# A two-layer hybrid decoder trunk on one core: input sums of the fast FFN tiles emitted earlier, and four low weight parts per layer by accumulating transfers

## The chip, the cores and the metric

The kernel runs on one core of one Trainium2 chip. The metric is the device time of one execution in microseconds (us), lower is better. The profile's span is the time from the first to the last instruction of one profiled execution.

## The reference, cut to what matters

A trunk of two layers over 528 positions (16 learned ones, then 512 of input) and 1024 channels. Each layer normalises, mixes with three recurrent head groups, projects and adds; then it normalises again and runs a gated MLP with a short convolution. The change touches the MLP alone:

```
def conv_glu_ffn(h, w_up, conv_w, conv_b, w_down):
    u = causal_dwconv(jnp.einsum('btd,df->btf', h, w_up), conv_w, conv_b)   # 3 taps
    gate, val = jnp.split(u, 2, axis=-1)                                    # 2816 each
    return jnp.einsum('btf,fd->btd', jax.nn.silu(gate) * val, w_down)

for l in range(DEPTH):                                                      # DEPTH = 2
    h = h + hybrid_mixer(rmsnorm(h, norm_mix_g[l]), ...)
    h = h + conv_glu_ffn(rmsnorm(h, norm_ffn_g[l]), ffn_w_up[l], ffn_conv_w[l],
                         ffn_conv_b[l], ffn_w_down[l])
return rmsnorm(h, final_norm_g)[:, N_META:]
```

All of it is float32.

## The kernel before, in words

**Products.** Every float32 operand is cut in two parts of a shorter type, high and low, and a product is three matmuls: high by high, low by high, high by low (names end in h and l: `wh`, `wl` for weights, `xh`, `xl` for the normalised input, `ah`, `al` for activations, `th`, `tl` for the sums below). Activations lie with channels on the 128 partitions and positions along the free dimension, in two halves of 264 (258 in the second layer). A weight tile is 128x1024 (512 KB): eight blocks of 128 input channels.

**Cutting (`split`, L420 to L427).** ACT casts the source to the high part (L421). Then DVE subtracts it from the source (L427). With `by_dma` ACT writes the negated source, rounded, into the low part (L424) and POOL issues an accumulating transfer that adds the source to it (L425); DVE has no part in that.

**Weights.** `raw_src` lists what SP fetches in order, `items` what is cut, in the order of use. An item of kind `p` is cut with DVE, `q` by transfer. A raw tile lies in one of three buffers `raw` until its cutting is done, a cut tile in one of four pairs `wh`, `wl` until PE is done with it. `take()` hands out the next item and first emits the cutting of those up to three ahead (`prep(i + 3)`), which emits the fetches of those after.

**The MLP.** 22 tiles of 128 gate channels with 128 value channels, j = 0 to 21. Tiles 0 to 3 and 21 are plain (`up_pair`): a gate unit and a value unit, each with two halves of eight blocks of three matmuls. Tiles 0 and 1 run as one block of four units, first half and then second half. A half's result is copied from PSUM by ACT (L1035) and its last tap taken (L1005) into two buffers u and c; then DVE adds the other two taps (`conv`, L1000), ACT applies silu (L1017), DVE multiplies (L1022), and the product is cut into `ah`, `al`.

Tiles 4 to 20 are fast (`up_fast`, `pair_products`): a two by two scheme with seven block products in place of eight. It wants four sums of the normalised input per pair of channel blocks, called T1 to T4, for four pairs a = 0 to 3. `sum_pair(a)` makes them once per layer: DVE puts high and low together for both blocks (L1049, two buffers), makes T1 and T2 (L1055, L1056) and then T3 and T4 (L1059, L1060), a buffer for each two, and each is cut into `th`, `tl` by transfer. All these buffers, u, c and those of the sums, are of one tag `t` with seven buffers (`TM = 7`); one that a transfer reads is free when the transfer has landed. The fast tile uses T1 in its third product, T2 in its fourth, which adds onto the PSUM of its first, once ACT has copied that out (L1077), and T3 and T4 later. Between its products lie the down projection's units of the group of tiles before it; their weights come by the ring `rd` (256 KB) and are cut by transfer already.

**Order.** PE and SP run in the order in which the program is written. For DVE, ACT and POOL a scheduler settles the order when the program is built: an instruction emitted earlier goes first among those that are ready, and a buffer goes to the one that gets there first. On the chip each engine then keeps that order. `sum_pair(0)` is emitted behind tile 1, pairs 1 and 2 behind tile 2, pair 3 behind tile 3.

Of the kernel before, what the change touches and what calls it, by code (L numbers as in the profile page):

```python
# [19 lines left out]
KD = D // P  # L20
# [10 lines left out]
NFF = 22  # L31

GROUPS = ((0, 4), (4, 8), (8, 12), (12, 16), (16, 22))
FAST = range(4, 21)
DOWNS = ((), (2, 2, 2, 2), (2, 2, 2, 2), (2, 2, 2, 2), (2, 2, 2, 1, 1, 0))
TM = 7
Q0 = 12
MAXH = 2
# [55 lines left out]
def hybrid_trunk_kernel(ctx, tc, x, w_in, w_out, w_up, w_down, par, pre_in, lru_w, kon, msk, rope, out):  # L94
# [105 lines left out]
    raw_src, items = [], []  # L200
# [4 lines left out]
        group[f"x{j}"], group[f"y{j}"], group[f"s{j}"] = [M_LX + j], [M_LY + j], [M_RG + j]  # L205
    orders = [[m for k in o.split() for m in group[k]] for o in (ORDER, ORDER1)]

    def plain(src, kn, ring="raw"):
        raw_src.append((src, kn, ring))
        items.append(("p" if ring == "raw" else "q", len(raw_src) - 1, kn))  # L210

    for l in range(DEPTH):
        for m in orders[l]:
            plain(w_in[l, m], KD)
        for m in range(KD):
            plain(w_out[l, m], KD)

        for g, (k0, k1) in enumerate(GROUPS):
            rows = iter(range(KD))
            for i, j in enumerate(range(k0, k1)):  # L220
                down = [next(rows) for _ in range(DOWNS[g][i] if g else 0)]
                if j in FAST:
                    raw_src.extend((w_up[l, r], KD, "raw") for r in (j, NFF + j))
                    ri = len(raw_src) - 2
                    items.extend((k, ri, KD) for k in "ab")
                    for q, m in enumerate(down):
                        plain(w_down[l, m, :, slice(*GROUPS[g - 1]), :], 4, "rd")
                        if q == 0:
                            items.append(("c", ri, KD))
                    if not down:  # L230
                        items.append(("c", ri, KD))
                    items.append(("d", ri, KD))
                else:
                    plain(w_up[l, j], KD)
                    plain(w_up[l, NFF + j], KD)
        for m in range(KD):
            plain(w_down[l, m, :, k0:k1, :], k1 - k0)
    raws, ready, sums = {}, {}, {}
# [256 lines left out]
    def whole(hi, lo):  # L495
        return lambda t0, n: (hi[:, t0:t0 + n], lo[:, t0:t0 + n])
# [406 lines left out]
    def layer(l):  # L903
# [86 lines left out]
        phase[0].release()  # L990
        phase[0], n_t[0] = tc.alloc_tile_pool(name=f"mlp{l}", bufs=1), TM
        c0 = META if lastl else 0
# [33 lines left out]
        def up_pair(j):  # L1026
            us = {}

            def ev(key, m):

                def f(i, t0, n, ps):
                    if key not in us:
                        us[key] = new_u()
                    u, c = us[key]
                    S.copy(u[:, 2 + t0:2 + t0 + n], ps[:, 0:n])  # L1035
                    o = max(t0, c0)
                    tap(u, c, m, o, t0 + n, ps[:, o - t0:n])
                return f
            return [(None, ev("g", j), lambda: gate(j, us)), (None, ev("v", NFF + j), lambda: value(j, us))]
# [4 lines left out]
        def sum_pair(a):  # L1044

            y = []
            for k in (2 * a, 2 * a + 1):
                y.append(big())
                V.tensor_tensor(y[-1][:, 0:2 * hn], xh[:, k, h0:T].bitcast(F32), xl[:, k, h0:T].bitcast(F32), op=ALU.add)  # L1049
            (b11, b12), (b21, b22) = ((t[:, 0:hn], t[:, hn:2 * hn]) for t in y)  # L1050
            for i in (0, 2):
                t = big()
                p0, p1 = t[:, 0:hn], t[:, hn:2 * hn]
                if i == 0:
                    V.tensor_tensor(p0, b11, b12, op=ALU.subtract)  # L1055
                    V.scalar_tensor_tensor(p1, p0, -1.0, b22, op0=ALU.mult, op1=ALU.subtract)  # L1056
                    t2 = p1
                else:
                    V.tensor_tensor(p0, b22, b12, op=ALU.subtract)  # L1059
                    V.scalar_tensor_tensor(p1, t2, -1.0, b21, op0=ALU.mult, op1=ALU.subtract)  # L1060
                split(t[:, 0:2 * hn].rearrange("p (h t) -> p h t", t=hn), *(x[:, a, i:i + 2, 0:hn] for x in tsum),
                      by_dma=True)
# [7 lines left out]
        def up_fast(j, halves):  # L1070
            us = {k: new_u() for k in "gv"}
            ug, uv = (us[k][0][:, 2 + h0:2 + T] for k in "gv")

            def evac(what, ps):
                p = ps[:, 0:hn]
                if what == "c11":
                    S.copy(ug[:, 0:hn], p)  # L1077
                elif what == "u":
                    S.copy(ug[:, hn:2 * hn], p)
                elif what == "q5":  # L1080
                    S.activation(uv[:, hn:2 * hn], p, AF.Copy, scale=-1.0)
                elif what == "c11b":
                    V.tensor_tensor(ug[:, 0:hn], ug[:, 0:hn], p, op=ALU.add)
                elif what == "c12":
                    V.tensor_tensor(ug[:, hn:2 * hn], ug[:, hn:2 * hn], p, op=ALU.add)  # L1085
                    u, c = us["g"]
                    tap(u, c, j, c0, T, u[:, 2 + c0:2 + T])
                    gate(j, us)
                elif what == "v":
                    V.tensor_tensor(uv[:, hn:2 * hn], uv[:, hn:2 * hn], p, op=ALU.subtract)  # L1090
                else:
                    S.activation(uv[:, 0:hn], p, AF.Copy, scale=-1.0)
                    u, c = us["v"]
                    tap(u, c, NFF + j, c0, T, u[:, 2 + c0:2 + T])
                    value(j, us)
            cut_at = (len(halves) + 1) // 2

            def between(i):
                for f in (halves[:cut_at], halves[cut_at:])[i]:
                    f()  # L1100
            pair_products(xs_fast, KD // 2, hn, evac, between)

        def down_halves(m, xs):

            w = []

            def f(t0, n):
                if not w:
                    w.append(take())
                ps = ps_mm.tile([P, 512], F32, tag="mm", name=nm("mm"))  # L1110
                product(w[0], xs, t0, n, range(len(xs)), ps, True, True)
                resid(m)(0, t0, n, ps)
            return [lambda t0=t0, n=n: f(t0, n) for t0, n in hd]

        for g, (k0, k1) in enumerate(GROUPS):
            rows = iter(range(KD))
            prev = [whole(*act[k]) for k in range(*GROUPS[g - 1])] if g else []
            for i, j in enumerate(range(k0, k1)):
                halves = [f for _ in range(DOWNS[g][i] if g else 0) for f in down_halves(next(rows), prev)]
                if j in FAST:  # L1120
                    up_fast(j, halves)
                else:
                    if j == 0:
                        run_units([u for i_ in range(2) for u in up_pair(i_)], xs_norm, hv, first=4)
                    elif j > 1:
                        run_units(up_pair(j), xs_norm, hv)
                    if j in (1, 2, 3):
                        for a in {1: (0,), 2: (1, 2), 3: (3,)}[j]:
                            sum_pair(a)

        def final(t0, n):
# [27 lines left out]
    with tc.manual_schedule(engines={mybir.EngineType.PE, mybir.EngineType.SP}):  # L1159
# [132 lines left out]
        for l in range(DEPTH):  # L1292
            layer(l)
# [106 lines left out]
```

## Time and profile before

| | us |
|---|---|
| median of 3 runs (1286.71 to 1287.97) | 1287.32 |
| the profiled execution | 1288.41 |
| its span | 1286.5 |
| PE busy | 1258.5 (98%) |
| DVE busy | 988.6 (77%) |
| ACT busy | 752.0 (58%) |
| POOL busy | 79.5 (6%) |
| mean granted clock of TensorE | 0.987 |

Busy times are sums over the span. The first layer's MLP runs from about 276 us, its first fast tile from about 324; in the second layer these are about 910 and 958. The granted clock is a share of full speed: 1.00 is 2.4 GHz and 0.50 is 1.2 GHz.

### The profile page before, as it was taken

Reading aid. Unit: us, or ns where it says so; the run is one execution under the profiler, and the core shown is the slowest. Engines: PE = TensorE matmul, PEld = TensorE weight load, DVE = VectorE, ACT = ScalarE, POOL = GpSimd, SP = SyncE. Lnnn points to the kernel's source line nnn. Section 1 sums busy time; section 2 is a strip of 40 time slices with the busy share of each in tenths; the row PEclk is TensorE's granted clock in tenths of the full one; section 3 lists DMA queues with packets and bytes.
Section 4 is the critical chain, followed back from the end, with each engine's and each line's share of the span. In section 5 each row is a group of like instructions: output and inputs, shape, how many; then the busy total and the mean of one; then the engine's idle time right before and its main releaser. Section 6 shows DMA issues by size and latency. Waiting matters only on the chain.

```text
span 1286.5 us, 25758 instructions
## 1 busy us (share of the span) xinstructions
PE 1258.5 (98%) x10244; PEld 1245.9 (97%) x10244; DVE 988.6 (77%) x1946; ACT 752.0 (58%) x1442; POOL 79.5 (6%) x179
## 2 busy tenths in 40 slices
PE   9999999999899999999999999999999999999997
PEld 8999999999899999999999999999989999999996
DVE  7987676468788888887588767764896888888865
ACT  6665555347666666666456645553684666666652
POOL 0000000001211111100000000000021111111000
PEclk8999999999899999999999999999998999999998
DMA  5322312324555445544232223122265555555422
GB/s 197 98 78 67 100 50 66 99 67 122 126 132 132 131 128 136 132 124 115 75 99 67 66 66 100 50 83 66 87 136 139 132 132 131 132 137 135 111 88 74
DMA packets 53240, 135.32 MB, mean 105 GB/s; under 512 B 5632, under 2 KB 12288, under 8 KB 53120
## 3 DMA queue, kind: packets, MB, share of 16 engines
q1 hardware_dynamic: 39424, 110.46, 27.5%
q0 software_dynamic: 12544, 21.06, 9.7%
q10 hardware_dynamic: 1152, 2.16, 0.5%
q8 instruction: 80, 1.31, 0.4%
q14 instruction: 40, 0.33, 0.1%
HBM read 110.51 MB, written 2.10 MB: 88 GB/s over the span
## 4 chain that ended last, share of the span: by engine, by line
PE 86%; DVE 6%; ACT 3%; DMA 3%; issue 1%; SPq 0%; POOL 0%; DVEq 0%; ACTq 0%; POOLq 0%
PE mm L130 63%; PE mx L130 23%; DMA tl<-t 2%; DVE t L1000 1%; PE mx L137 1%; DVE wl L427 1%; DVE t L567 1%; DVE t L1138 0%; DMA raw<-in_w_in_dram 0%; DVE sc L591 0%; ACT wh L421 0%; ACT th L421 0%; DMA mk<-in_msk_dram 0%; DVE t L870 0%; ACT sc L674 0%
## 5 line engine op out<-in xcount | busy, mean ns | idle before, releaser
L130 PE MATMUL mm<-xh,wh 128*128 128x264 f32 (+1 forms) x1424 | 417.9, 293 | 0.8 <-ACT xh L421 0.8
L130 PE MATMUL mm<-xl,wh 128*128 128x264 f32 (+1 forms) x1424 | 404.3, 284 | 0.7 <-DVE xl L427 0.3
L130 PE MATMUL mm<-xh,wl 128*128 128x264 f32 (+1 forms) x1424 | 403.4, 283 | 0.0
L130 PE MATMUL mm<-ah,wh 128*128 128x264 f32 (+2 forms) x960 | 273.2, 285 | 0.0
L130 PEld LDWEIGHTS mm<-xl,wh 128*128 128x128 f32 x1424 | 268.8, 189 | 3.7 <-issue 1.9
L130 PE MATMUL mm<-al,wh 128*128 128x264 f32 (+2 forms) x960 | 272.4, 284 | 0.0
L130 PE MATMUL mm<-ah,wl 128*128 128x264 f32 (+2 forms) x960 | 272.1, 283 | 0.0
L130 PEld LDWEIGHTS mm<-xh,wh 128*128 128x128 f32 x1424 | 268.5, 189 | 3.6 <-issue 2.0
L130 PEld LDWEIGHTS mm<-xh,wl 128*128 128x128 f32 x1424 | 268.6, 189 | 0.2 <-DVE wl L1195 0.2
L427 DVE TENSOR_TENSOR wl<-raw,wh 128x1024 fp32r<-128x1024 f32 (+2 forms) x168 | 182.5, 1088 | 82.2 <-ACT wh L421 81.7
L421 ACT CAST wh<-raw 128x1024 fp32r<-128x1024 f32 (+2 forms) x168 | 158.3, 942 | 149.2 <-PE mm L130 143.6
L130 PEld LDWEIGHTS mm<-ah,wh 128*128 128x128 f32 x960 | 182.0, 190 | 0.1
L130 PEld LDWEIGHTS mm<-al,wh 128*128 128x128 f32 x960 | 181.9, 189 | 0.1
L130 PEld LDWEIGHTS mm<-ah,wl 128*128 128x128 f32 x960 | 181.9, 189 | 0.0
L1000 DVE SCALAR_TENSOR_TENSOR t<-t,pr,t 128x528 f32<-128x528 f32 (+1 forms) x176 | 132.7, 757 | 11.1 <-ACT t L1005 5.1
L130 PE MATMUL mx<-th,wh 128*128 128x264 f32 (+1 forms) x408 | 117.2, 287 | 0.0
L130 PE MATMUL mx<-th,wl 128*128 128x264 f32 (+1 forms) x408 | 116.6, 286 | 0.0
L130 PE MATMUL mx<-tl,wh 128*128 128x264 f32 (+1 forms) x408 | 116.3, 285 | 0.0
L1005 ACT ACTIVATE t<-t,pr 128x528 f32<-128x528 f32 (+1 forms) x68 | 56.0, 823 | 58.5 <-DVE t L1085 56.5
L427 DVE TENSOR_TENSOR wl<-ss,wh 128x1024 fp32r<-128x1024 f32 x68 | 83.0, 1221 | 4.6 <-ACT wh L421 1.8
L425 POOL DMA_DIRECT2D wl<-rd x64 | 56.6, 884 | 448.6 <-ACT wl L424 384.4
L130 PEld LDWEIGHTS mx<-tl,wh 128*128 128x128 f32 x408 | 78.3, 192 | 0.0
(231 smaller groups left out, 2170.9 us busy)
## 6 DMA issues: line engine op xcount, KB each, us to landing
raw<-in_w_up_dram SPq DMA_DIRECT2D x88, 512.0 KB, 3.6
raw<-in_w_in_dram SPq DMA_DIRECT2D x52, 512.0 KB, 3.6
rd<-in_w_down_dram SPq DMA_DIRECT2D x64, 256.0 KB, 2.7
wl<-rd POOLq DMA_DIRECT2D x64, 256.0 KB, 3.6
raw<-in_w_out_dram SPq DMA_DIRECT2D x16, 512.0 KB, 3.5
raw<-in_w_down_dram SPq DMA_DIRECT2D x16, 384.0 KB, 3.1
hT<-in_x_dram SPq DMA_DIRECT2D x4, 528.0 KB, 5.4
t<-in_rope_dram ACTq DMA_DIRECT2D x8, 264.0 KB, 3.3
```

Of the source, the lines that this page charges most:

```text
L130: PE.matmul(o, a, b, start=start, stop=stop, **kw)
L137: PE.transpose(o, a, ident[0:n, 0:n])
L421: S.copy(hi, src)
L425: G.dma_start(lo, src, accum_op=ALU.add)
L427: V.tensor_tensor(lo, src, hi.bitcast(F32), op=ALU.subtract)
L567: V.tensor_tensor(o, a, b, op=ALU.mult)
L1000: V.scalar_tensor_tensor(c[:, 0:cn], u[:, i + c0:i + c0 + cn], pr[l][:, w + i:w + i + 1], c[:, 0:cn], op0=ALU.mult, op1=ALU.add)
L1005: S.activation(c[:, a - c0:b - c0], src, AF.Identity, bias=pr[l][:, C_FB + m:C_FB + m + 1], scale=pr[l][:, C_FW + 3 * m + 2:C_FW + 3 * m + 3])
```

## The change

`sum_pair` of pairs 0 and 1 is emitted behind tile 1, of pairs 2 and 3 behind tile 2, and none behind tile 3. The gate and value weights of tiles 2 and 3 (four tiles of 128x1024 per layer) become items of kind `q`: their low part is made by ACT's negated copy and an accumulating transfer of 512 KB. They stay on the ring `raw`.

```
+SENT = (2, 3)
...
-    def plain(src, kn, ring="raw"):
+    def plain(src, kn, ring="raw", by_dma=False):
         raw_src.append((src, kn, ring))
-        items.append(("p" if ring == "raw" else "q", len(raw_src) - 1, kn))
+        items.append(("q" if by_dma else "p", len(raw_src) - 1, kn))
...
-                        plain(w_down[l, m, :, slice(*GROUPS[g - 1]), :], 4, "rd")
+                        plain(w_down[l, m, :, slice(*GROUPS[g - 1]), :], 4, "rd", True)
...
-                    plain(w_up[l, j], KD)
-                    plain(w_up[l, NFF + j], KD)
+                    plain(w_up[l, j], KD, by_dma=j in SENT)
+                    plain(w_up[l, NFF + j], KD, by_dma=j in SENT)
...
-                    if j in (1, 2, 3):
-                        for a in {1: (0,), 2: (1, 2), 3: (3,)}[j]:
+                    if j in (1, 2):
+                        for a in {1: (0, 1), 2: (2, 3)}[j]:
                             sum_pair(a)
```

## Rows read from the trace of the kernel before

**Rows 1.** The page's first part: busy time of each engine, its share of the span and the count of instructions.

```profile
PE 1258.5 (98%) x10244; PEld 1245.9 (97%) x10244; DVE 988.6 (77%) x1946; ACT 752.0 (58%) x1442; POOL 79.5 (6%) x179
```

**Rows 2.** PE's waits over the whole span, longest first: who waited for what, us in total, how often, the longest.

```profile
PE mm L130 <- DMA tl<-t: 9.0, 2, 4.8
PE mm L130 <- ACT th L421: 2.5, 2, 1.5
PE mx L130 <- DVE acc L442: 2.0, 2, 1.2
```

**Rows 3.** The timeline of PE at the first fast tile, two rows of each layer: start, duration, the instruction, and in brackets the idle time before it and what ended it.

```profile
329.41 0.39 PE L130 MATMUL mm<-th,wh 128*128 128x264 f32 x1 [1.04 <-ACT th L421]
334.03 0.59 PE L130 MATMUL mm<-tl,wh 128*128 128x264 f32 x1 [4.23 <-DMA tl<-t]
...
962.82 0.39 PE L130 MATMUL mm<-th,wh 128*128 128x258 f32 x1 [1.46 <-ACT th L421]
967.98 0.58 PE L130 MATMUL mm<-tl,wh 128*128 128x258 f32 x1 [4.78 <-DMA tl<-t]
```

**Rows 4.** Windows around the first fast tile in both layers: the stretch and its length, busy time and instructions of PE, weight loads, DVE, ACT and POOL, granted clock, DMA share, GB/s.

```profile
292.00:328.00 36.00, 36.00 (x299) 36.00 (x298) 34.22 (x54) 29.07 (x54) 6.58 (x11) 1.00 0.55 133
...
334.00:339.05 5.05, 5.02 (x23) 5.02 (x24) 0.69 (x1) 1.29 (x3) 0.05 (x1) 0.50 0.59 101
339.05:345.00 5.95, 5.95 (x50) 5.95 (x50) 3.10 (x6) 2.23 (x3) 0.00 (x0) 0.99 0.51 147
...
968.00:974.00 6.00, 6.00 (x28) 6.00 (x29) 0.74 (x2) 1.28 (x3) 0.00 (x0) 0.50 0.71 134
974.00:980.00 6.00, 6.00 (x52) 6.00 (x52) 3.83 (x7) 2.81 (x3) 0.00 (x0) 0.99 0.41 117
```

**Rows 5.** The chain of work that ended last, two pieces of 300 to 340 us and one of 935 to 975: start, length, what.

```profile
309.81 5.58 DMA tl<-t
...
330.23 3.75 DMA tl<-t
...
963.59 4.35 DMA tl<-t
```

**Rows 6.** Windows of 6 us ahead of the first fast tile of the first layer; the columns are those of rows 4.

```profile
300.00:306.00 6.00, 6.00 (x52) 6.00 (x51) 5.96 (x10) 3.97 (x8) 0.10 (x1) 1.00 0.51 164
306.00:312.00 6.00, 6.00 (x52) 6.00 (x51) 6.00 (x12) 5.28 (x11) 1.96 (x3) 1.00 0.43 106
312.00:318.00 6.00, 6.00 (x51) 6.00 (x51) 6.00 (x10) 3.28 (x7) 0.00 (x0) 1.00 0.81 204
318.00:324.00 6.00, 6.00 (x52) 6.00 (x51) 6.00 (x13) 5.93 (x13) 2.38 (x5) 1.00 0.53 90
324.00:330.00 6.00, 4.76 (x37) 4.34 (x36) 6.00 (x11) 6.00 (x13) 2.33 (x5) 1.00 0.77 134
```

**Rows 7.** The timeline of DVE: the first and the last of the four subtractions for the weights of tiles 2 and 3 in the first layer, the first of what stands ahead of pair 3's L1056 there, and that L1056 in both layers.

```profile
293.33 1.22 DVE L427 TENSOR_TENSOR wl<-raw,wh 128x1024 fp32r<-128x1024 f32 x1 [2.38 <-ACT wh L421]
...
308.26 1.21 DVE L427 TENSOR_TENSOR wl<-raw,wh 128x1024 fp32r<-128x1024 f32 x1
...
323.26 0.67 DVE L292 TENSOR_TENSOR ss<-raw 128x512 f32<-128x512 f32 x1
323.86 0.75 DVE L1000 SCALAR_TENSOR_TENSOR t<-t,pr,t 128x528 f32<-128x528 f32 x1
...
328.14 0.43 DVE L1056 SCALAR_TENSOR_TENSOR t<-t,t 128x264 f32<-128x264 f32 x1
...
961.68 0.42 DVE L1056 SCALAR_TENSOR_TENSOR t<-t,t 128x258 f32<-128x258 f32 x1
```

**Rows 8.** Groups of ACT's instructions from 292 to 329 us, shapes kept apart: busy us, mean ns of one, idle time before them.

```profile
L421 ACT CAST wh<-raw 128x1024 fp32r<-128x1024 f32 x5 | 5.2, 1050 | 2.9 <-PE mm L130 2.9
L421 ACT CAST th<-t 128x528 fp32r<-128x528 f32 x7 | 4.4, 629 | 2.7 <-DVE t L1056 2.7
...
L424 ACT ACTIVATE tl<-t 128x528 fp32r<-128x528 f32 x6 | 3.9, 643 | 0.0
```

**Rows 9.** Accumulating transfers into tl: the issues on POOL and the time from issue to landing over the whole span (16 transfers), then landing times of those issued from 308 to 310, from 942 to 945 and from 323 to 327 us (two each).

```profile
L425 POOL DMA_DIRECT2D tl<-t x16: 856/1090/1632, 308.7 to 965.8; - x16
DMA to landing us min/median/max: 3.3/3.8/6.6
...
DMA to landing us min/median/max: 5.2/5.4/5.6
...
DMA to landing us min/median/max: 6.0/6.3/6.6
...
DMA to landing us min/median/max: 3.3/3.3/3.4
```

**Rows 10.** The timeline of ACT in the first layer: the casts of tile 2's weights, which wait for a buffer that PE gives up, and a cast of a sum.

```profile
292.25 1.05 ACT L421 CAST wh<-raw 128x1024 fp32r<-128x1024 f32 x1 [1.79 <-PE mm L130]
...
295.17 1.05 ACT L421 CAST wh<-raw 128x1024 fp32r<-128x1024 f32 x1 [1.12 <-PE mm L130]
...
317.69 0.63 ACT L421 CAST th<-t 128x528 fp32r<-128x528 f32 x1 [2.72 <-DVE t L1056]
```

**Rows 11.** SP's issues of weight fetches in the first layer, the first and the last of four: start, duration, what.

```profile
294.58 0.33 SPq L249 DMA_DIRECT2D raw<-in_w_up_dram  x1
...
309.53 0.33 SPq L249 DMA_DIRECT2D raw<-in_w_up_dram  x1
```

## The prediction

> **What bounds the kernel now.** I read the page's busy shares first: PE is busy for 98% of the span [rows 1]. So the only time to be had, short of fewer matmuls, is the little that PE waits and the time in which it runs at its lower clock. The list of PE's waits comes next [rows 2]. Of its entries two belong to the place that the change touches: 9.0 us for a transfer into tl and 2.5 us for the cast into th, two waits each, which is one per layer. They are 11.5 us of PE's idle time, and every other entry is 2.0 us or less.
>
> The timeline of PE shows where they lie [rows 3]. In layer 0 the first fast tile (tile 4) starts its T1 product; its first three row pairs run, then PE waits 1.04 us for th of the last pair, does one matmul, and waits 4.23 us for tl of the same pair. In layer 1 the same two waits take 1.46 and 4.78 us. In stretches around them the granted clock falls [rows 4]: from 334.00 to 339.05 it is 0.50, the lower of the two levels (1.2 of 2.4 GHz), and 23 matmuls take 5.05 us, where 50 take 5.95 us right behind it. 23 × 0.119 = 2.74 us, so 2.31 us are lost. In layer 1 it is 0.50 from 968 to 974, 28 matmuls in 6.00 us against 52 in 6.00: 28 × 0.115 = 3.23, so 2.77 us are lost. Waits and clock together are 11.5 + 5.1 = **16.6 us**: the most that this change can return, unless it touches something else.
>
> Why the last tl is late I read from the chain of waits in that stretch [rows 5] and the windows of 6 us [rows 6]: DVE is busy 6.00 of 6.00 us in each one from 306 to 330, while ACT has 2.72 us to spare in 312 to 318. The chain goes through DVE's convolutions (L1000) and the sums (L1055, L1056) and ends in a 3.75 us transfer issued at 330.23. It holds a second transfer, 5.58 us from 309.81: a "t" buffer (there are seven) that pair 1 needed was held until pair 0's tl had landed. So the wait has three parts in series: DVE's backlog, buffers held by transfers, the last transfer itself.
>
> **The change part by part.**
>
> *Low parts off DVE.* The weights of tiles 2 and 3 are four per layer. Each loses one DVE subtraction, 1.22 us, at 293.33, 296.25, 301.17 and 308.26 in layer 0 [rows 7]: 4 × 1.22 = 4.9 us off an engine that is the bottleneck from about 299 on. The first two lie partly beside idle DVE time (2.38 us idle before the first), but the later two don't, and the convolutions behind the first two start earlier as far as ACT lets them.
>
> *Sums ahead of tiles.* Pair 1's sums now precede tile 2, pair 3's precede tile 3, in priority on DVE, ACT and POOL. Ahead of pair 3's L1056 (328.14) DVE now does three convolution steps of tile 3 (323.86, 325.14, 327.46, spaced 0.68) and two weight sums of tile 5 (0.60 each) [rows 7]: 2.0 + 1.2 = 3.2 us that can go behind it. By DVE alone, then, this sum ends at 328.57 − 4.9 − 3.2 = 320.5.
>
> *ACT.* Each of the four gets a negated copy of 128x1024. The trace has none of that size; the casts of that size take 1050 ns, and at 128x528 the negated copy (643 ns) is as long as the cast (629 ns) [rows 8]. So 4 × about 1.0 = 4.1 us more work. ACT is busy 29.07 of the 36 us from 292 to 328 [rows 4]; it would be 33.1. The cover is thin, so I take nothing for it on PE, but part of it as a delay of the sums (below). Bounds: nothing lost, if the copies fall into the 6.9 idle us, to all 4.1 us late.
>
> *Four transfers of 512 KB.* None of this kind and size is in the trace. From both sides: a single one of 264 KB lands 3.3 us after its issue at best, 6.6 at worst; two of them issued together (528 KB, 308.75) land after 5.2 and 5.6 us, in layer 1 after 6.0 and 6.6 [rows 9]. The pair is nearest, so 6.0 us, with 3.3 to 13.2 (twice the worst) as ends. First use: the cast of tile 2's first weight runs at 292.25, its copy would end at 294.3, its transfer land at 300.4. PE frees a buffer every 2.92 us (292.25, 295.17) [rows 10], so eight half units of 2.92 us end at 292.2 + 3 × 2.92 = 301.0 and tile 2 begins there, wanting this low part with its third matmul at 301.3. The margin is 0.9 us. The next three land near 304, 308 and 312 and are wanted at 307, 313 and 319; their margins grow. Cost on PE: nothing; price if it is late: the lateness, plus about 2.5 us if the clock falls.
>
> *SP's queue.* A raw buffer (there are three) is now freed when its transfer lands and no longer when DVE's subtraction ends. The fetches at 294.58, 297.50, 302.41 and 309.53 [rows 11] move to about 300, 304, 308 and 312, and the two fetches of tile 4's partner rows behind the third move with it. The last weight of tile 3 is then cast near 305 and wanted at 319, tile 4's weights at 324.5 and 327: hidden. POOL issues four more transfers; behind one that still waits for ACT stand the tl transfers of pairs 0 and 1, which are not ready before 306.
>
> *The last transfer.* From L1056's end to the issue of its tl transfer are 330.23 − 328.57 = 1.7 us. I add 3 us to 320.5 for "t" buffers and ACT together: each pair holds two for a transfer's length, pairs 0 and 1 want eight in a row and there are seven, and the one such hold that the chain shows is 5.6 us against a DVE that had other work. So issue at 325.2; a landing of 5.0 us (the middle of 3.3 and 6.6) gives 330.2. PE wants th at 329.41 − 1.04 = 328.4 [rows 3] and tl right after. **A wait of 1.8 us is left** where 5.27 were, and in layer 1, worked in the same way (L1056 ends at 962.1, the issue is 1.5 us later at 963.59 [rows 5, 7]; 962.1 − 4.9 − 3.2 + 3 + 1.5 + 5.0 = 963.5, against 962.82 − 1.46 = 961.4 with 0.1 for the matmul between), 2.0 us where 6.24 were. Whether a wait of 2 us lowers the clock no row here shows; a wait of 1.04 us stands alone for only one matmul. I take that it does not.
>
> The Trainium skill ("DMA: Bandwidth & Descriptors", section on the anatomy of a SWDGE DMA) has a fit of 2.0 us plus the bytes over 436 GB/s; as an estimate from it 264 KB land after 2.6 us, and then no wait would be left and the sum would be the full 16.6 us. The trace disagrees: its fastest such transfer takes 3.3 us.
>
> What is late next, if this wait is gone, is T2, which needs the copy out of the first product (L1077), done at 329.80 on an ACT that was full; with 328.7 as its new due time this is within a microsecond and part of the same 1.8.
>
> **Sum.** 16.6 − 1.8 − 2.0 = 12.8 us. The profiled execution took 1288.41 us, of which 1286.5 are the span; 1288.41 − 12.8 = 1275.6. It lies 1.09 above the median of the runs, so against 1287.32 the forecast is **1274.5 us**.
>
> **The rivals.**
>
> *ACT takes DVE's place.* For it: 33.1 of 36 us busy, and ACT's order is fixed, so an idle stretch that waits for DVE (2.72 us at 317.69 [rows 10]) is not simply filled. Against: the four copies are early, at 293 to 306, and the window from 300 to 306 has 2.0 us free [rows 6]. If the whole 4.1 us come back as delay, layer 0's last tl lands at about 331 to 332 rather than 330.2, the wait is some 3 us, and the clock falls as it does now: each layer returns 2 to 3.5 us. 1287.3 − 6 = 1281.
>
> *Nothing comes of it: the buffers.* Seven "t" buffers for two pairs in a row (eight) and tile 2's four: tile 2's results must leave PSUM by 312.8, when the fifth half unit from there wants one of four PSUM buffers. If pairs 0 and 1 hold all seven past that, PE waits there instead, and a wait of about 4 us with its clock only moves. 1287. For it: the hold in the chain [rows 5]. Against: tile 0's and tile 1's buffers come free from 296 to 307, and only four can hang on a transfer at a time.
>
> *Slower: the transfers follow one another too slowly.* PE uses one of the four weights per 5.85 us. If a 512 KB transfer takes 8.5 us and they go one behind the other, the first is 1.5 us late and each of the next three 2.65 more: 9.5 us, with a fall of the clock 12 per layer. The sums get that time too, so the 8.3 us of now are gone: +3.7 per layer, 1295. It decides from 5.85 us per transfer on. For it: two of 264 KB took 6.6 us in layer 1. Against: that includes the fixed part, and in 318 to 327 single ones landed after 3.3 us [rows 9].
>
> The Trainium skill ("SBUF — State Buffer", "SBUF: two separate sides") says that DVE in a two-port mode locks GpSimd out and starves such transfers of descriptors. By that rule the transfers would be slowest just where DVE is full, and the slower case would be the likeliest. The trace speaks against it: with DVE busy 6.00 of 6.00 us from 318 to 330, POOL's issues took 0.86 to 1.2 us and landings 3.3 us.
>
> **How the numbers follow.** Forecast 0.62 (own range 1270 to 1279), ACT 0.16, the buffers 0.10, slower 0.12. Less than all of 16.6 us can hardly be beaten: 1287.3 − 16.6 = 1270.7, so the low end is 1270. The high end takes in the ACT case with its spread, 1285; the rest, 0.2, lies above. What this kernel's runs can tell from no change is 0.2%, 2.6 us: faster 0.78, within 0.09 (most of the buffers case), slower 0.13.
>
> **What would show it.** Right: PE's waits on tl and th fall from 11.5 us to under 5, the granted clock stays at 1.00 behind the start of tile 4, DVE has no subtraction into wl from raw between 293 and 309, and pair 3's L1056 ends by 324. Wrong: a PE wait on a transfer wl<-raw at tile 2's start (first step of the 512 KB part); a PE wait on t or a PSUM evacuation by ACT near 313 (buffers); pair 3's th waiting on ACT work with DVE idle (ACT); or a wait of the old length with the sums ahead of it done early, which would mean that the transfer alone, and not DVE's backlog, set it.

## The result, and the profile after

The changed kernel takes 1302.91 us (median of 3 runs, 1302.85 to 1303.00) against 1287.32: a ratio of 1.0121, 95% interval 1.0098 to 1.0144. It is slower by 15.6 us; the forecast was 1274.5. Its profiled execution has a span of 1301.1 us, 14.6 more than before. Where these lie is in the first part of the page (busy time, share of the span and instructions of each engine), which answers to [rows 1]:

```profile
PE 1264.0 (97%) x10244; PEld 1250.3 (96%) x10244; DVE 981.1 (75%) x1938; ACT 758.9 (58%) x1450; POOL 86.3 (7%) x187
```

PE has the same 10244 instructions, is busy 1264.0 − 1258.5 = 5.5 us longer, and is idle 37.1 us (1301.1 − 1264.0) where it was 28.0: 9.1 + 5.5 = 14.6. The longer busy time goes with the clock: it is 0.66 to 0.90 in the last four windows below, where [rows 6] have 1.00 in each. DVE lost its eight subtractions and ACT gained eight copies, as said, so the load did move. PE's waits over the span (who waited for what, us in total, times, longest), against [rows 2]:

```profile
PE mm L131 <- DMA wl<-raw: 9.6, 2, 5.2
PE mm L131 <- ACT t L1006: 6.3, 3, 2.7
PE mx L131 <- DVE dg L466: 2.4, 2, 1.2
...
PE mm L131 <- DMA tl<-t: 1.9, 1, 1.9
...
PE mm L131 <- ACT ah L422: 1.5, 1, 1.5
```

(Most line numbers are one higher than before: L131 was L130, L422 was L421, L1006 was L1005.) The 11.5 us of waits for th and tl have come down to 1.9. In their place stand two waits that the kernel before did not have: a low part made by transfer, once per layer, and results leaving PSUM (L1006), those of tile 2 in the first layer. The timeline of PE shows them in the first layer and the first of them in the second; they lie a tile and more ahead of the place of [rows 3]:

```profile
311.42 0.59 PE L131 MATMUL mm<-xh,wl 128*128 128x264 f32 x1 [4.37 <-DMA wl<-raw]
322.01 0.39 PE L131 MATMUL mm<-xh,wh 128*128 128x264 f32 x1 [2.67 <-ACT t L1006]
...
953.52 0.58 PE L131 MATMUL mm<-xh,wl 128*128 128x258 f32 x1 [5.24 <-DMA wl<-raw]
```

The windows of 6 us over the stretch that [rows 6] show before (columns as there: PE, weight loads, DVE, ACT, POOL, granted clock, DMA share, GB/s):

```profile
300.00:306.00 6.00, 6.00 (x52) 6.00 (x51) 5.64 (x10) 4.36 (x9) 0.00 (x0) 1.00 0.32 87
306.00:312.00 6.00, 1.63 (x11) 1.42 (x10) 4.31 (x10) 6.00 (x11) 4.15 (x5) 0.77 0.71 131
312.00:318.00 6.00, 6.00 (x37) 6.00 (x36) 0.00 (x0) 1.65 (x4) 1.99 (x5) 0.66 1.03 184
318.00:324.00 6.00, 3.33 (x24) 3.11 (x23) 2.48 (x4) 3.46 (x7) 0.00 (x0) 0.90 1.07 276
324.00:330.00 6.00, 6.00 (x43) 6.00 (x43) 5.60 (x12) 2.47 (x5) 0.00 (x0) 0.81 0.69 205
```

PE does 11, 37 and 24 matmuls in three windows where it did 52, 51 and 52. DVE, 6.00 us busy in each of them before, does nothing at all from 312 to 318. And the DMA engines, 0.32 busy from 300 to 306, are full from 312 on. An idle DVE beside full transfers is the opposite of the shortage that the change set out to mend: the work waits for data, and the data waits for something that came late.

What came late stands in the timeline of ACT:

```profile
293.83 1.05 ACT L425 ACTIVATE wl<-raw 128x1024 fp32r<-128x1024 f32 x1
295.06 1.05 ACT L422 CAST wh<-raw 128x1024 fp32r<-128x1024 f32 x1 [0.17 <-PE mm L131]
...
299.19 1.04 ACT L422 CAST wh<-raw 128x1024 fp32r<-128x1024 f32 x1
...
303.88 1.05 ACT L422 CAST wh<-raw 128x1024 fp32r<-128x1024 f32 x1 [1.64 <-DMA raw<-in_w_up_dram]
304.85 0.63 ACT L1018 ACTIVATE t<-t 128x528 f32<-128x528 f32 x1
305.38 1.99 ACT L425 ACTIVATE wl<-raw 128x1024 fp32r<-128x1024 f32 x2
...
309.94 1.04 ACT L425 ACTIVATE wl<-raw 128x1024 fp32r<-128x1024 f32 x1
...
320.44 1.04 ACT L422 CAST wh<-raw 128x1024 fp32r<-128x1024 f32 x1 [6.79 <-DMA raw<-in_w_up_dram]
321.39 1.03 ACT L1006 ACTIVATE t<-mm,pr 128x264 f32<-128x264 f32 x2
```

L422 is a weight's cast, L425 its negated copy. The first copy stands close behind its cast. The second and third do not: the casts of their weights end at 296.1 and 300.2, the copies run at 305.38, behind the fourth cast and a silu. And the fourth cast waits for a fetch. The issues on POOL and on SP, and the chain of waits, close the circle. POOL's timeline:

```profile
295.20 1.00 POOL L426 DMA_DIRECT2D wl<-raw  x1 [18.77 <-PE mm L131]
306.74 1.78 POOL L426 DMA_DIRECT2D wl<-raw  x2 [10.54 <-DVE t L1060]
...
311.28 0.86 POOL L426 DMA_DIRECT2D wl<-raw  x1
...
313.68 0.86 POOL L426 DMA_DIRECT2D tl<-t  x1 [0.21 <-ACT t L1036]
```

SP's timeline, two of its issues of weight fetches:

```profile
300.19 0.33 SPq L250 DMA_DIRECT2D raw<-in_w_up_dram  x1
...
311.43 0.33 SPq L250 DMA_DIRECT2D raw<-in_w_up_dram  x1
```

The DMA queues from 306 to 324 us (packets, MB, share of all 16 engines; then issues, KB each and median us to landing):

```profile
q0 software_dynamic: 835, 2.35, 75.5%
...
wl<-raw POOLq DMA_DIRECT2D x3, 512.0 KB, 6.4
raw<-in_w_up_dram SPq DMA_DIRECT2D x3, 512.0 KB, 9.0
tl<-t POOLq DMA_DIRECT2D x4, 264.0 KB, 10.6
```

Read together: transfer 1 is issued at 295.20. It lands after 4.9 us, and at 300.19 SP may at last reuse its raw buffer. The fetch takes 3.7 us, so cast 4 starts at 303.88, and behind it copy 2 at 305.38. Transfer 2 is issued at 306.74 and lands 4.6 us later at 311.34; PE's matmul, ready at 311.42 − 4.37 = 307.05, starts at 311.42. Meanwhile transfers 2, 3 and 4 come in one bunch with the four tl of pairs 0 and 1 and the held fetches. The fetch that SP issues at 311.43 takes 9.0 us, not 3.7. The cast that wants it sits on ACT from 313.65 to 320.44, ahead of the evacuation of tile 2 (L1006, 321.39), for which PE then waits until 322.01. The last tl of the bunch takes 13.38 us, and DVE's next sum waits for its buffer:

```profile
313.68 13.38 DMA tl<-t
```

That row is of the chain of waits; before, the longest such piece was 5.58 us in the first layer [rows 5] and 5.99 us in the second. The second layer repeats the late copies and the wait for wl some 640 us later. Its two waits for L1006, 1.8 us each, come later than tile 2 there, at the first fast tile (975.84 and 979.34).

### The profile page after: what moved, and what is told of

It is laid out like the page before. It is cut to its first block, busy times and chain, and to the rows that moved or that the text cites. A ratio compares the mean times of both kernels' runs of the same rounds, so it can differ in the third digit from the quotient of the medians.

```text
span 1301.1 us, 25777 instructions
## 1 busy us (share of the span) xinstructions
PE 1264.0 (97%) x10244; PEld 1250.3 (96%) x10244; DVE 981.1 (75%) x1938; ACT 758.9 (58%) x1450; POOL 86.3 (7%) x187
## 4 chain that ended last, share of the span: by engine, by line
PE 84%; DVE 7%; DMA 4%; ACT 3%; issue 1%; SPq 0%; DVEq 0%; ACTq 0%; POOLq 0%
PE mm L131 61%; PE mx L131 22%; DMA tl<-t 1%; DMA raw<-in_w_up_dram 1%; PE mx L138 1%; DVE t L568 1%; DVE wl L428 1%; DVE t L1001 1%; DVE t L1139 0%; DMA raw<-in_w_in_dram 0%; ACT wl L425 0%; DVE sc L592 0%; DMA wl<-raw 0%; ACT tl L425 0%; DVE t L1050 0%
## 5 line engine op out<-in xcount | busy, mean ns | idle before, releaser
L131 PE MATMUL mm<-xh,wh 128*128 128x264 f32 (+1 forms) x1424 | 421.7, 296 | 5.3 <-ACT t L1006 4.5
L131 PE MATMUL mm<-xh,wl 128*128 128x264 f32 (+1 forms) x1424 | 407.3, 286 | 9.6 <-DMA wl<-raw 9.6
L131 PE MATMUL mm<-xl,wh 128*128 128x264 f32 (+1 forms) x1424 | 407.7, 286 | 0.5 <-DVE xl L428 0.3
L131 PEld LDWEIGHTS mm<-xh,wl 128*128 128x128 f32 x1424 | 272.2, 191 | 10.2 <-DMA wl<-raw 10.0
L131 PEld LDWEIGHTS mm<-xh,wh 128*128 128x128 f32 x1424 | 272.2, 191 | 8.4 <-ACT t L1006 4.9
L131 PEld LDWEIGHTS mm<-xl,wh 128*128 128x128 f32 x1424 | 272.3, 191 | 3.6 <-issue 1.9
L131 PE MATMUL mm<-ah,wh 128*128 128x264 f32 (+2 forms) x960 | 273.1, 284 | 1.5 <-ACT ah L422 1.5
L131 PE MATMUL mm<-al,wh 128*128 128x264 f32 (+2 forms) x960 | 272.4, 284 | 0.5 <-DVE al L428 0.5
L131 PE MATMUL mm<-ah,wl 128*128 128x264 f32 (+2 forms) x960 | 272.2, 284 | 0.0
L422 ACT CAST wh<-raw 128x1024 fp32r<-128x1024 f32 (+2 forms) x168 | 158.3, 942 | 160.3 <-PE mm L131 141.1
L428 DVE TENSOR_TENSOR wl<-raw,wh 128x1024 fp32r<-128x1024 f32 (+2 forms) x160 | 172.9, 1082 | 79.0 <-ACT wh L422 78.6
L131 PEld LDWEIGHTS mm<-ah,wh 128*128 128x128 f32 x960 | 181.7, 189 | 1.8 <-ACT ah L422 1.7
L131 PEld LDWEIGHTS mm<-al,wh 128*128 128x128 f32 x960 | 181.5, 189 | 0.9 <-DVE al L428 0.8
L131 PEld LDWEIGHTS mm<-ah,wl 128*128 128x128 f32 x960 | 181.7, 189 | 0.0
L131 PE MATMUL mx<-th,wh 128*128 128x264 f32 (+1 forms) x408 | 116.8, 286 | 0.4 <-ACT t L1078 0.4
L131 PE MATMUL mx<-th,wl 128*128 128x264 f32 (+1 forms) x408 | 116.2, 285 | 0.0
L131 PE MATMUL mx<-tl,wh 128*128 128x264 f32 (+1 forms) x408 | 115.8, 284 | 0.0
L1006 ACT ACTIVATE t<-t,pr 128x528 f32<-128x528 f32 (+1 forms) x68 | 56.0, 824 | 59.2 <-DVE t L1086 57.1
L131 PEld LDWEIGHTS mx<-th,wh 128*128 128x128 f32 x408 | 77.7, 190 | 0.6 <-ACT t L1078 0.6
```

Of the source, the lines that this page charges most:

```text
L131: PE.matmul(o, a, b, start=start, stop=stop, **kw)
L422: S.copy(hi, src)
L428: V.tensor_tensor(lo, src, hi.bitcast(F32), op=ALU.subtract)
L1006: S.activation(c[:, a - c0:b - c0], src, AF.Identity, bias=pr[l][:, C_FB + m:C_FB + m + 1], scale=pr[l][:, C_FW + 3 * m + 2:C_FW + 3 * m + 3])
```

## The experiments

Each kernel ran beside the kernel before on the same chip; the median of the kernel before there (1287.8 to 1288.4) is given with each, and the ratio with its 95% interval. The theories: **A**, ACT's order holds copies 2 and 3 back; **B**, transfers and raw ring are too slow in any order; **C**, the sums' new place takes the "t" buffers.

**The sums alone.** All low parts on DVE again.

```diff
-SENT = (2, 3)
+SENT = ()
```

> The sums moved alone, all low parts of tiles 2 and 3 by DVE as before. Three theories of the 15.6 us that the change costs. A, ACT's order: the copies of the 2nd to 4th weight stand on ACT behind the 4th cast, which waits for a raw tile fetched only after the 1st transfer has landed, so three transfers of 512 KB go out in a bunch with the tl transfers. B, the transfers and the ring of three raw buffers are too slow in any order. C, the sums moved ahead take the t buffers from tile 2's results. A and B: no loss without the transfers; DVE loses only the 3.2 us that go behind the sums, about half of the 5.7 us by which the last tl is late now: 1277 to 1287 us. C: most of the loss stays, 1296 us or more.

Measured: 1285.40 against 1288.40, ratio 0.9976 (0.9966 to 0.9986), 3.0 us faster, in the range of A and B. PE's waits have no entry for a transfer into wl any more, and the two at the first fast tile are short:

```profile
PE mm L131 <- DMA tl<-t: 2.9, 2, 2.2
PE mm L131 <- ACT t L1006: 2.6, 2, 1.5
```

So the sums' new place is no loss, which speaks against C as the cause. The other half costs 15.6 + 3.0 = 18.6 us where it is added to it.

**The low parts alone.** The sums where they were before.

```diff
-                    if j in (1, 2):
-                        for a in {1: (0, 1), 2: (2, 3)}[j]:
+                    if j in (1, 2, 3):
+                        for a in {1: (0,), 2: (1, 2), 3: (3,)}[j]:
```

> The four low parts by transfer alone, the sums where they were. A and B: PE's waits on wl<-raw stay (4.4 and 5.2 us) and the time is about that of the changed kernel, 1297 to 1306 us. C: without the moved sums the loss is gone, 1275 to 1287 us.

Measured: 1309.27 against 1288.40, 1.0160 (1.0145 to 1.0175), 20.9 us slower and above the 1306 of A and B. Both kinds of wait are there, for wl from raw (9.0 us, two) and for th and tl (18.0 us, five). The copies held back are in this kernel too (2 and 3 run at 304.91, behind cast 4 at 303.41), so it is not the moved sums that hold them back.

**Copies behind their casts.** The changed kernel, with a high priority for the negated copy of the four weights. On ACT copies 1 and 2 then stand directly behind their casts, 3 and 4 ahead of theirs.

```diff
-                ready[i] = cut_in_two(r[:, 0:n], n, by_dma=kind == "q")
+                ready[i] = cut_in_two(r[:, 0:n], n, by_dma=(2 if raw_src[ri][2] == "raw" else 1) if kind == "q" else 0)
...
-            S.activation(lo, src, AF.Copy, scale=-1.0)
+            with tc.high_priority(400) if by_dma == 2 else nullcontext():
+                S.activation(lo, src, AF.Copy, scale=-1.0)
```

> The changed kernel with each negated copy of the four weights given high priority, so that on ACT the 2nd copy stands directly behind the 2nd cast and the 3rd ahead of the 3rd cast. A: the 2nd transfer leaves at about 297.5 in place of 306.7 us and lands by 303, before PE wants it at 307; no PE wait on wl<-raw; 1275 to 1289 us. B: transfers and fetches remain as slow, PE still waits 4 us or more for a transfer or for what stands behind a late fetch; 1295 us or more. C: 1296 or more too, but with the wait on a PSUM evacuation near 313 and not on wl.

Measured: 1295.20 against 1288.40, 1.0053 (1.0038 to 1.0068). The second transfer leaves at 298.48 in place of 306.74 (POOL's timeline):

```profile
298.48 0.86 POOL L427 DMA_DIRECT2D wl<-raw  x1 [1.92 <-ACT wl L426]
```

The wait for wl is gone, and 15.6 us of loss became 6.8. A named the cause of that wait rightly, and order alone was worth 8.8 us. But A's range was missed and B's number held. The wait that C had named came too, near C's number: PE now waits twice for tile 2's evacuation:

```profile
PE mm L131 <- ACT t L1007: 14.8, 2, 7.9
```

ACT's timeline shows what it waited for ahead of it, the raw fetch and then a "t" buffer:

```profile
306.79 1.06 ACT L426 ACTIVATE wl<-raw 128x1024 fp32r<-128x1024 f32 x1 [2.82 <-DMA raw<-in_w_up_dram]
...
318.61 0.38 ACT L1037 COPY t<-mm 128x264 f32<-128x264 f32 x1 [4.39 <-DMA tl<-t]
```

The fourth weight's fetch, issued at 300.26 beside transfers 2 and 3, took 6.5 us. It puts transfer 4 at 308.15; pair 0's tl, issued at 311.02 behind it, takes 7.5 us and keeps the "t" buffer that tile 2's copy wants. Two theories for what is left: **R**, the raw ring's late fetches; **T**, too few "t" buffers, which is C again for what A leaves over.

**Only tile 3's weights by transfer.**

```diff
-SENT = (2, 3)
+SENT = (3,)
```

> The changed kernel with only tile 3's two weights by transfer; those of tile 2 by DVE. The fetch of the 4th weight then follows DVE's subtraction of the 1st, at about 294.5, and no cast on ACT waits for a transfer; ACT's order has each copy right behind its cast without being told. A: no PE wait on wl<-raw, last tl earlier by 2.4 us of DVE and 3.2 of the order: 1275 to 1284 us. B: half of the transfers, half of the loss: 1292 to 1297 us. C: 1296 us or more.

Measured: 1287.00 against 1288.40, 0.9989 (0.9980 to 0.9999). No wait for wl; two of 2.2 and 2.0 us for L1006. It is 1.6 us worse than no transfers at all (runs of 1285.69 to 1287.74 against 1284.24 to 1286.87), with half of DVE's relief: neither A's range (1275 to 1284) nor B's (1292 to 1297).

**No wait for the raw ring.** The third experiment, with two of the four weights fetched into two buffers of another ring (`ss`, idle there). It was meant to leave no fetch that waits for a landing.

```diff
-                    plain(w_up[l, j], KD, by_dma=j in SENT)
-                    plain(w_up[l, NFF + j], KD, by_dma=j in SENT)
+                    plain(w_up[l, j], KD, "ss" if j == 3 else "raw", by_dma=j in SENT)
+                    plain(w_up[l, NFF + j], KD, "ss" if j == 2 else "raw", by_dma=j in SENT)
...
+            elif ring == "ss":
+                r = own("ss", 2, (P, KD * P))
```

> The kernel with the copies given priority, and besides the 2nd and 3rd of the four weights fetched into the two buffers of the weight sums, which stand empty until tile 4, so that no fetch waits for a transfer. What the priority left over (1295.2 against 1288.4 us) is for theory R, the ring: the 4th weight's copy on ACT waits 2.8 us for a fetch that waits for the 1st transfer, and all behind it is late. For theory T, the t buffers: pair 0's tl transfer stands behind 512 KB ones on the queue (7.5 us to landing), and tile 2's results wait for its buffer on ACT. R: the PE wait on a PSUM evacuation (7.9 and 6.9 us) goes, 1278 to 1288 us. T: it stays at 4 us or more, 1291 us or more.

Measured: 1290.39 against 1287.99, 1.0024 (1.0013 to 1.0035). Another 4.4 us are back, near the 1278 to 1288 of R and below T's 1291, inside neither. The wait for the evacuation is halved (3.6 and 3.7 us). The chain and DVE's timeline say what remains of it:

```profile
299.29 6.44 DMA raw<-in_w_up_dram
...
305.81 0.69 DVE ss L295
```

```profile
305.81 0.69 DVE L295 TENSOR_TENSOR ss<-raw 128x512 f32<-128x512 f32 x1 [3.94 <-DMA raw<-in_w_up_dram]
```

The fetch of tile 4's weights meets three 512 KB transfers (DMA share 1.01 from 300 to 306) and takes 6.4 us; DVE, whose order is fixed, stands 3.94 us before their sum.

The edit did not do all that was meant. It frees the fetches of the four weights, but both fetches of tile 4's weights still wait for landings of transfers 1 and 4, as SP's waits from 285 to 330 us show:

```profile
SPq L252 <- DMA wl<-raw: 27.7, 2, 17.7
```

The first leaves at 299.29, where the kernel with the sums alone sends it at 298.58; so for this fetch the 6.4 us in place of 3.6 weigh more than the later start, but R is not removed whole. And DVE's wait is again one of order: with the sums alone the same instruction runs late enough that a landing at 305.73 would not have held it (DVE's timeline there):

```profile
314.22 0.68 DVE L293 TENSOR_TENSOR ss<-raw 128x512 f32<-128x512 f32 x1
```

**The third experiment with the sums in their old places.**

```diff
-                    if j in (1, 2):
-                        for a in {1: (0, 1), 2: (2, 3)}[j]:
+                    if j in (1, 2, 3):
+                        for a in {1: (0,), 2: (1, 2), 3: (3,)}[j]:
```

> The copies given priority, the sums at their old places (pair 1 behind tile 2, pair 3 behind tile 3). T: with pair 1 no longer ahead of tile 2 for the t buffers the wait on tile 2's evacuation goes or falls under 3 us; the wait for the last tl stays at 4 to 10 us as in the run of low parts alone; 1286 to 1293 us. R: the evacuation's wait stays as it is, 7 us, and the tl wait is added: 1300 us or more.

Measured: 1299.10 against 1287.99, 1.0090 (1.0075 to 1.0105), between T (1286 to 1293) and R (1300 and more). The wait near 313 shrank to 0.41 us, as T had it, but a later one for an evacuation (3.74 us, at 330.87) and waits for th and tl of 14.9 us are there. By themselves the low parts cost 11.1 us even in the good order.

**Which pair gains.** From the sums alone, only pair 1 moved behind tile 1 (pair 3 behind tile 3 as before), and then only pair 3 moved behind tile 2:

```diff
-                    if j in (1, 2):
-                        for a in {1: (0, 1), 2: (2, 3)}[j]:
+                    if j in (1, 2, 3):
+                        for a in {1: (0, 1), 2: (2,), 3: (3,)}[j]:
```

> Sums moved alone, low parts by DVE, but only pair 1 earlier: pairs 0 and 1 behind tile 1, pair 2 behind tile 2, pair 3 behind tile 3. If the gain of the sums moved alone (1285.4 against 1288.4) comes from pair 3 going ahead of tile 3's convolutions on DVE, this one gives nothing, 1287 to 1290 us. If it comes from the t buffers that pair 1 gets earlier, it keeps the gain, 1284 to 1286.5 us.

```diff
-                        for a in {1: (0, 1), 2: (2, 3)}[j]:
+                        for a in {1: (0,), 2: (1, 2, 3)}[j]:
```

> Sums moved alone, low parts by DVE: pair 0 behind tile 1, pairs 1, 2 and 3 behind tile 2, so only pair 3 is earlier than before. If the gain comes from pair 3 ahead of tile 3's convolutions it is kept: 1284 to 1286.5 us. If it comes from pair 1, nothing: 1287 to 1290 us.

Measured: pair 1 early 1292.71 against 1287.99, 1.0041 (1.0026 to 1.0056), 4.7 us slower; pair 3 early **1281.72**, 0.9957 (0.9942 to 0.9971), 6.3 us faster, the fastest of all. The first is slower than both its ranges, the second faster than both: pair 3 has the gain, and pair 1's earlier place is a loss. The two halves of the move pull against each other, and −6.3 + 4.7 = −1.6 lies near the −3.0 of both, within the intervals. PE's waits with pair 1 early, and with pair 3 early:

```profile
PE mm L131 <- DMA tl<-t: 8.8, 3, 4.3
PE mm L131 <- ACT th L422: 6.7, 2, 3.4
```

```profile
PE mm L131 <- ACT t L1006: 2.4, 3, 1.1
PE mm L131 <- DMA tl<-t: 2.3, 2, 1.5
```

With pair 3 early its L1057 (the L1056 of [rows 7]) starts 4.0 us sooner than the 328.14 of before, and no transfer was changed:

```profile
324.15 0.41 DVE L1057 SCALAR_TENSOR_TENSOR t<-t,t 128x264 f32<-128x264 f32 x1
```

**An eighth "t" buffer.** It fits only where other buffers are given up, so a control gives these up alone, from the kernel with pair 1 early:

```diff
-    def half(tag="hs", bufs=4):
+    def half(tag="hs", bufs=3):
...
-        ss, sd, rs = (big("sm", 9, (P, 20)) for _ in range(3))
+        ss, sd, rs = (big("sm", 5, (P, 20)) for _ in range(3))
```

> The control of the run before: the same fewer half and small buffers, but seven t buffers. Both theories: the loss of pair 1 stays, 1291 to 1296 us; what lies above 1292.7 is the price of the buffers given up.

The same with the buffer, and then pair 3 early with the buffer:

```diff
-TM = 7
+TM = 8
```

> Pair 1 alone earlier (the run that took 1292.7 against 1288.0 us), with eight t buffers in place of seven; room for it is made by three in place of four half buffers and five in place of nine of the small statistics. Theory T8: pair 1 ahead of tile 2 costs because two pairs and a tile want more than seven t buffers, each held until a tl transfer lands; with eight the loss goes, 1284 to 1289 us. Rival D: it costs because on DVE pair 1's seven steps go ahead of tile 2's convolutions; the number of buffers changes nothing, 1291 us or more.

> Pair 3 alone earlier (1281.7 against 1288.0 us) with eight t buffers, half and small buffers as above. T8: the waits left at the first fast tile (2.6 and 3.3 us in the two layers), of which some come from results that wait for a t buffer, shrink: 1278 to 1281.5 us. D: no change beside the price of the buffers given up, 1281 to 1286 us.

Measured against 1287.79: control 1297.67, above the 1291 to 1296 expected, so what is given up costs 1297.67 − 1292.71 = 5.0 us; with the buffer 1293.11, so the buffer returns 4.6 where pair 1 is early. Where only pair 3 is, 1286.23 is 4.5 above 1281.72; if the price is the same 5.0 there, the buffer returns 0.5. That pair 1 made early runs short of buffers fits this. But T8's two ranges were missed (1284 to 1289 and 1278 to 1281.5), and 12.6 us of waits for th and tl stay with pair 1 early even with eight, so it is not the whole of its loss; what the rest is stays open. The price in that second order was not run by itself.

**The buffer under the "no wait for the raw ring" kernel.** T8 stands for the buffer, F for DVE's wait on the fetch of tile 4's weights.

```diff
-TM = 7
+TM = 8
```

> The four low parts by transfer with copies given priority and fetches freed (1290.4 against 1288.0 us), with eight t buffers. T8: the wait on tile 2's evacuation (3.6 and 3.7 us) falls under 1.5 us and the time to 1283 to 1287 us. Rival F: that wait comes from DVE, where a weight sum of tile 4 waits for a fetch that takes 6.4 us beside the transfers; it stays at 3 us or more, 1288 us or more.

Measured: 1291.30 against 1287.79, 1.0027 (1.0017 to 1.0036), as without it. DVE waits 3.89 us for the same fetch at 305.34, PE 6.5 us for L1009. F's number held. But in the first layer PE's wait fell from 3.56 to 1.24 us with DVE's wait as long as before, and in the second it rose from 3.73 to 4.93, so DVE's wait alone does not set it. Here too the price of what was given up is in the number.

## Why the prediction was wrong, step by step

*"What bounds the kernel now"* held. The waits for th and tl can be removed by order alone: with only pair 3 moved they and what replaced them shrink from 11.5 to 5.9 us (2.4 and 2.3 above, and 1.2 for the copy out of the first product, L1078, which the prediction had called late next), the granted clock averages 0.991 for 0.987, and 6.3 us come back. The ceiling of 16.6 us was never near.

*"Sums ahead of tiles"* was right in its mechanism and half right in its parts. I costed pair 3's gain (3.2 us of DVE work behind its sum; measured 4.0 us sooner) and let pair 1's earlier place cost only a share of the 3 us of delay added for "t" buffers and ACT together. By itself it costs 4.7 us of time; the mis-sized term is that one. Part of it is the buffers.

*"Low parts off DVE"* was right as far as DVE goes, eight subtractions fewer. What that was worth by itself no run shows, since the transfers came with it; together they were no gain: with tile 3's two alone the kernel was 1.6 us slower than with the sums alone.

*"ACT"* is the step that failed first. It costed the copies well (1.0 us estimated, 1.04 measured), and then put each directly behind its cast: "the next three land near 304, 308 and 312" rests on this alone. The built program puts copies 2 and 3 behind cast 4; why the scheduler did so no run shows. I had followed what happens to the fetch (to "about 300": it came at 300.19) and to who needs the fetched weight ("cast near 305 and wanted at 319 ... hidden"), but not what stands behind that cast on ACT. There stood the copies themselves, the sums' casts and tile 2's evacuations. So "SP's queue", called hidden, became the path: landing 1, fetch, cast 4, copies 2 and 3, transfers 2 and 3. Putting them in order returned 8.8 of the 18.6 us that the low parts cost beside the moved sums, and freeing the fetches of the four weights another 4.4.

*"Four transfers of 512 KB"*, "Cost on PE: nothing". The landings of the first two were shorter than my 6.0 us: 4.9 and 4.6. The first was in time; the third and fourth, in the bunch, took 6.4 and 11.6. What the step left out is what they do to others. The kernel's accumulating queue took 0.114 × 1301.1 = 148.3 us of 16 engines where it took 0.097 × 1286.5 = 124.8, so each of the eight takes some 2.9 us of all of them. The rows are of the pages' third part, after and before:

```profile
q0 software_dynamic: 13696, 25.25, 11.4%
...
q0 software_dynamic: 12544, 21.06, 9.7%
```

Three in a row beside four tl (6.9 to 13.4 us each; 5.2 to 5.6 for those two of before [rows 9]) and beside fetches of 512 KB are a full DMA for 12 us. With the order and the fetches of the four weights mended, what stays against the sums alone is 2.4 + 3.0 = 5.4 us. In that kernel the place is a fetch of 6.4 us in front of DVE's sum; that this accounts for all 5.4 was not shown, since no run moved the fetch or the sum alone. So how much of the 5.4 is the price of the transfers in any order, and how much one more place in an engine's order, stays open.

*The rivals.* The slower one had the sign and the place, a wait for wl from raw at tile 2, but not the reason: it decides from 5.85 us per transfer, and transfers 1 and 2 took less; 3 and 4 took more, but PE did not wait for them. Its number, 1295, is near that of the kernel with the copies in order (1295.2) for other reasons. "ACT takes DVE's place" counted busy time; ACT was busy 1.65 us of the 6 from 312 on and late because of its order. "The buffers" called a wait on an evacuation near 313, and that is what the kernel with the copies in order shows: 7.9 us, from 313.7 to 321.6.

*The rule on DVE and GpSimd* that I weighed in the prediction (the Trainium skill, "SBUF — State Buffer", section "SBUF: two separate sides") is not what came true, and I had applied it too widely: its part "Who interferes with whom" says that `tensor_tensor`, which much of DVE's work here is, has no two-port mode. The slowest tl of the first layer, 13.38 us, fell where DVE was idle for 6 us on end and the DMA share was 1.03. For the price of one transfer, the fit in the Trainium skill ("DMA: Bandwidth & Descriptors", anatomy of one SWDGE DMA) gives an estimate of 2.0 + 1.2 = 3.2 us for 512 KB; the trace disagrees, with 4.6 and 4.9 us.

## What to carry to other kernels

Work moved from an engine to a transfer also moves the moment at which its source buffer comes free: follow that buffer to the next fetch, the fetch to the instruction that waits for it, and then read everything that stands behind this instruction in its engine's fixed order. Price a transfer twice, by its own landing and by the share of all DMA engines that it takes from those beside it. And where a change has two parts, ask of each what it does alone: here one line of order, a pair's sums emitted one tile earlier, is faster than both kernels (1281.72 us).

## What was not expected of the hardware

A fetch of 512 KB, 3.6 to 3.7 us in the median of a whole span, took 6.4 to 9.5 us beside accumulating transfers in the first layer, and an accumulating transfer of 264 KB there up to 13.4 us, where 3.3 us was its best. An issue on POOL took 0.86 us for 264 KB and for 512 KB alike (313.68 and 311.28).
